# Four of eight row pairs of w_up by seven products in five chunks, with part of their sums made by transfers in HBM

## The chip, the cores and the metric

The kernel runs on one core of a Trainium2 chip. The metric is the device time of one execution in microseconds. Engines are named as in the profile: PE multiplies matrices, DVE and ACT work elementwise, POOL (GpSimd) does small work and issues some of the transfers, SP issues most transfers. Each engine takes its instructions in the order written; engines wait for each other by semaphores only.

## The reference

One layer on 256 tokens of width 2048, all in float32, one batch, one layer deep:

```
h = rmsnorm(x) * g1;  p = h @ W_in               # 2048 x 4160, columns for the two attentions
A = dilated-window attention, 8 heads of 128 ;  B = latent attention, 8 heads
x = x + rmsnorm(concat(A, B) @ W_out) * g2       # 2048 x 2048
h = rmsnorm(x) * g3
u = square(relu(h @ W_up))                       # 2048 x 8192
x = x + rmsnorm(u @ W_down) * g4                 # 8192 x 2048
```

The change is in the product with W_up, and in work that goes on beside the attention stages.

## The kernel before, in words

**Three passes.** A product of float32 matrices is made from parts: each operand is split into `hi`, its float32r rounding, and `lo`, the rest, and hi·hi, hi·lo and lo·hi are added in PSUM. A weight tile comes from HBM into one of five buffers `raw`; ACT writes `hi` (line 293, or 297 where a column of norm gains is multiplied in), DVE writes `lo` (line 294 or 298). There are eight buffers each of `hi` and `lo`; the class `Weights` emits a tile's load and split six tiles ahead of its use. So a split waits for the product eight tiles back, and a load on SP waits for the split five loads back.

**The product with w_up.** The 8192 columns are done in 16 chunks of 1024. A chunk runs over 16 row tiles of 128 (`k`), two token blocks `b` and two column halves, and adds into four PSUM banks; a plain tile takes 2 × 2 × 3 = 12 matmuls of 512 columns. Two neighbouring row tiles form a 2 × 2 block product, which Winograd's form of Strassen's scheme does with seven block products instead of eight: 21 matmuls instead of 24. In chunks 1 to 15 the pairs 0, 1 and 2 (row tiles 0 to 5) are done so, steps ("w", 0), ("w", 1), ("w", 2) of `UP_STEPS`; row tiles 6 to 15 are plain steps ("k", k). In chunk 0 all are plain.

**Right sums.** With the pair's rows `a` = (a0, a1) and `b` = (b0, b1), halves of 512 columns, the seven products need a0, b, t = (a0 + a1, a1 + b1) and u = (a0 + a1 + b1, a0 + a1 + b1 + b0). Both rows are loaded to a staging tile `ab` (of which there is one), by POOL except for the very first pair; DVE makes t and u in three additions (lines 345, 349, 350), and four tiles are split: a0 (512 columns), b, u, t.

**Left sums.** `left_sums` makes, once, the four sums of each pair of tiles of the normalized input hT, and writes the gain-scaled values back over hT; so from chunk 1 on, rows 0 to 5 need no gain in the split. This happens during the second half of chunk 0. The sums lie in the tile `st`.

**Closing.** Four further PSUM banks `m` collect the products that are shared between outputs; after the last pair of a chunk `close` combines them on DVE, and while the next chunk runs `up_evac` adds them to the accumulators (line 909), applies relu on ACT, transposes on PE (line 287) and squares on ACT.

**Order.** The program is written out by one pass of Python. `Flow` keeps a clock that counts the planned cost of the matmuls issued; side chains (generators) give waiting times with `yield`, and are resumed when that clock has passed. So an operation's place in an engine's order follows from planned times, while the engines themselves run as their waits allow. In the attention stages POOL has only a few small operations: the powers that make 1/rms (`rstd_pre`, `rstd_kv`, `rstd_q`, `rstd_pw`, line 485) and one memset.

Of the kernel before, what the change touches and what calls it, by code (L numbers as in the profile page):

```python
# [18 lines left out]
F32 = mybir.dt.float32  # L19
# [7 lines left out]
P = 128  # L27
# [11 lines left out]
FF = 4 * D  # L39
# [53 lines left out]
D_UP, UP_STEP = 1.8, 2.2  # L93


N_SEVEN, SUMS_AHEAD = 3, 2
UP_STEPS = [("k", k) for k in range(6, 11)]
for _i, _n in enumerate(((11, 12), (13,), (14, 15))):
    UP_STEPS += [("w", _i)] + [("k", k) for k in _n]


DOWN_SEVEN = ((7, 11, 13, 17, 19, 23, 25, 29), (4, 7, *range(9, 28, 2)))
# [148 lines left out]
def layer(nc, tc, io):  # L251
# [76 lines left out]
    def up_weight(j, k):  # L328
        return io["w_up"][k * P:(k + 1) * P, j * CW:(j + 1) * CW]

    late = {}

    def seven(load, targets):

# [28 lines left out]
    def seven_up(j, kp):  # L363
        def load():
            if j == FF // CW - 1 and kp:
                return [weights.load(up_weight(j, 2 * kp + i), CW, f"raw_w{j}_{kp}{i}") for i in range(2)]
            return load_two(late["ab"], nc.gpsimd if (j, kp) > (1, 0) else nc.sync,
                            io["w_up"][2 * kp * P:(2 * kp + 2) * P, j * CW:(j + 1) * CW])
# [30 lines left out]


    wide_u, after = [], 0
    for j in range(FF // CW):
        wide_u.append([])
        for what, k in [("k", k) for k in range(KD)] if j == 0 else UP_STEPS:
            if what == "k":
                ts = [weights.plan(up_weight(j, k), 1, CW, gcol[:, 8 + k:9 + k])]
# [124 lines left out]
    def prelude():  # L531
# [14 lines left out]
        nc.vector.reduce_sum(ss0, ss0h, axis=mybir.AxisListType.X)  # L546
        rstd0.append(rstd_of(ss0, NB, D, "pre"))

    def tables():

        yield D_TAB[0]
        nc.scalar.dma_start(out=pos_i, in_=io["pos"])
        nc.scalar.dma_start(out=cst, in_=io["consts"])
        yield D_TAB[1]
        pos_f = con.tile([P, NB], F32, name="pos_f")
        nc.vector.tensor_copy(pos_f, pos_i)
        ang = pa.tile([P, 2, NB, 96], F32, tag="qkT", bufs=2, name="ang")
# [12 lines left out]
        yield 4.0  # L570
        nc.scalar.activation(trig, ang, AF.Sin)
# [77 lines left out]

    pre = flow.start(prelude())  # L650
    tab = flow.start(tables())
    heads, evacs = [], []
    for half in range(2):
        qkv = {}
# [250 lines left out]
    def up_evac(j, b, i, acc, order, more=None):  # L905

        yield UP_STEP * order
        if more is not None:
            nc.vector.tensor_tensor(out=acc, in0=acc, in1=more, op=OP.add)
            yield 1.6  # L910
        r = late["up"].tile([P, 512], F32, tag="r", bufs=2, name=f"r{j}_{b}")
        nc.scalar.activation(r, acc, AF.Relu, scale=rstd2[b])
        yield D_UP if j > 1 else 2 * D_UP
        t = bank(i, f"rt{j}_{b}")
        for k in range(4):
            transpose(t[:, k * P:(k + 1) * P], r[:, k * P:(k + 1) * P])
# [41 lines left out]
    def left_sums(kp):  # L958

        up, k, tt = late["up"], 2 * kp, nc.vector.tensor_tensor  # L960
        f, q = [late["c"][:, i * 512:(i + 1) * 512] for i in range(2)]
        hs = [t[:, k:k + 2, :].rearrange("p k s -> p (k s)") for t in hT]
        tt(out=f, in0=hs[0].bitcast(F32), in1=hs[1].bitcast(F32), op=OP.add)
# [3 lines left out]
        st = [late["st"][:, i * 512:(i + 1) * 512] for i in (2 * kp, 2 * kp + 1)]  # L967
        yield 3.0
        for t, x in ((hs, f), (st, q)):
            nc.scalar.activation(t[0], x, AF.Copy)  # L970
        yield 1.5
        for t, x in ((hs, f), (st, q)):
            tt(out=t[1], in0=x, in1=t[0].bitcast(F32), op=OP.subtract)
        sums.append([[t[:, i * P:(i + 1) * P] for t in st] for i in range(4)])
        yield 0.5

    def all_sums():
        for kp in range(N_SEVEN - 1):
            yield from left_sums(kp)
        yield 8.0  # L980
        yield from left_sums(N_SEVEN - 1)

    def three(out, a, w, first, last):

# [3 lines left out]
    def seven_products(ts, left, accs, m, first, last):  # L988

        (a11, a12, a22), (s3, s1, s2, s4) = left  # L990
        prods = ((a11, 0, 0, 1), (a12, 1, 0, (0, 0)), (s4, 1, 1, (0, 1)), (s2, 2, 0, 6), (a22, 2, 1, (1, 0)),
                 (s3, 3, 1, 7), (s1, 3, 0, 5))
        for p, (a, i, half, to) in enumerate(prods):
            w = weights.get(ts[i])
# [21 lines left out]
    for j in range(FF // CW):  # L1016
# [9 lines left out]
        for t, b in order:  # L1026
            what, k, tiles = steps[t]
            if (j, t, b) == (0, 8, 0):
                flow.finish(*res)
                late["po"].release()  # L1030
                mix.release()
                late["up"] = pool("up", "right")
                late["st"] = late["up"].tile([P, 3 * CW], F32R, tag="st", bufs=1, name="st")
                for n in ("ab", "c"):
                    late[n] = late["up"].tile([P, 2 * CW], F32, name=n)
                flow.start(all_sums())
# [3 lines left out]
            if j == 1 and what == "w":  # L1040
                flow.until(lambda: len(sums) > k)
            if what == "k":
                w = weights.get(tiles[0])
                h_done(k, b)
                for n in range(2):
                    c = slice(n * 512, (n + 1) * 512)
                    three(accs[b, n], [tok(hT[x], k, b) for x in range(2)], [w[x][:, 0, c] for x in range(2)], t == 0, t == len(steps) - 1)
                    if j == 0 and t == len(steps) - 1:
                        evac.append(flow.start(up_evac(n, b, at[b, n], accs[b, n], 2 * b + n - 0.25 * (2 * b + n))))
                    flow.pump()  # L1050
                if b == NB - 1:
                    weights.free(tiles[0])
                continue

            first, last = k == 0, k == N_SEVEN - 1
# [208 lines left out]
```

## Time and profile before

| | |
|---|---|
| median of three runs | 1052.88 us (1051.48 to 1053.32) |
| the profiled execution | 1052.05 us, span 1050.3 us, mean granted clock 0.998 |
| busy: PE, DVE, ACT, POOL | 1039.0, 811.0, 625.4, 61.5 us |
| transfers | 229.34 MB, 218 GB/s over the span |
| attention stages and w_out | to about 363 us |
| w_up, chunk 0 | about 363 to 407 us, then a chunk each 43.4 us |

A row of the page's groups names line, engine, operation, what is written and read, the count, then busy time in us and the mean of one in ns, then idle time before it and what ended that. In a timeline the first two columns are start and length in us; a bracket gives the idle time of that engine before it and what ended it.

### The profile page before, as it was taken

What the parts mean: (1) busy time and instruction counts of PE and PEld (TensorE: products, weight loads), DVE (VectorE), ACT (ScalarE), POOL (GpSimd) and SP (SyncE); (2) the same over time, 40 slices, a digit from 0 to 9 for tenths busy, and PEclk for the clock granted to TensorE, in tenths of its full rate; (3) what the DMA queues carried; (4) which work ended last, traced back from release to release, by engine and by line L of the source; (5) the groups of instructions that cost most, each with busy time, mean ns of one, the idle gap of its engine ahead of it and who ended that gap; (6) DMA issues with size and microseconds to landing.
All of it is one profiled execution on the core that took longest, in us unless ns stands there. A gap on an engine that the chain in (4) does not pass through costs nothing.

```text
span 1050.3 us, 13459 instructions
## 1 busy us (share of the span) xinstructions
PE 1039.0 (99%) x4854; PEld 865.9 (82%) x4854; DVE 811.0 (77%) x1080; ACT 625.4 (60%) x834; POOL 61.5 (6%) x116
## 2 busy tenths in 40 slices
PE   9999999999999999999999999999999999999996
PEld 6888899888888788888888888888888888888885
DVE  6676536577557679879888798887899978989995
ACT  6675436565555467666665666666567564766661
POOL 0000000000000000010000000000000001112100
PEclk9999999999999999999999999999999999999999
DMA  8975447454447295646556465469788767788952
GB/s 298 371 230 155 140 127 239 141 166 155 141 170 234 77 344 174 224 143 238 194 189 201 145 234 194 151 227 319 246 276 315 267 223 259 268 300 313 381 186 81
DMA packets 80643, 229.34 MB, mean 218 GB/s; under 512 B 7616, under 2 KB 12224, under 8 KB 80192
## 3 DMA queue, kind: packets, MB, share of 16 engines
q1 hardware_dynamic: 65888, 176.45, 50.3%
q0 software_dynamic: 14112, 51.39, 14.2%
q8 instruction: 38, 0.62, 0.2%
q10 hardware_dynamic: 576, 0.64, 0.2%
q14 instruction: 29, 0.24, 0.1%
HBM read 212.72 MB, written 15.73 MB: 218 GB/s over the span
## 4 chain that ended last, share of the span: by engine, by line
PE 96%; DVE 1%; DMA 1%; issue 1%; ACT 0%; POOL 0%; DVEq 0%; POOLq 0%; ACTq 0%
PE y L283 26%; PE acc_u L283 26%; PE acc_o L283 8%; PE m L283 5%; PE md L283 5%; PE acc_v L283 4%; PE acc_qk L283 4%; PE acc_ckv L283 2%; PE acc_ukv L283 2%; PE acc_q L283 2%; PE acc_cq L283 2%; PE acc_k L283 2%; PE acc_uq L283 2%; PE rt L287 1%; PE sc_b L283 1%
## 5 line engine op out<-in xcount | busy, mean ns | idle before, releaser
L294 DVE TENSOR_TENSOR lo<-raw,hi 128x1024 fp32r<-128x1024 f32 (+3 forms) x213 | 241.7, 1152 | 91.5 <-ACT hi L293 90.7
L293 ACT ACTIVATE hi<-raw 128x1024 fp32r<-128x1024 f32 (+3 forms) x213 | 209.5, 999 | 77.6 <-PE y L283 20.8
L283 PE MATMUL acc_u<-hi,hT_hi 128*128 128x512 f32 x386 | 153.3, 397 | 0.0
L283 PE MATMUL acc_u<-hi,hT_lo 128*128 128x512 f32 x386 | 151.0, 391 | 0.4 <-DVE hT_lo L294 0.4
L283 PE MATMUL acc_u<-lo,hT_hi 128*128 128x512 f32 x386 | 150.7, 391 | 0.0
L283 PE MATMUL y<-hi,uhi 128*128 128x512 f32 x376 | 146.8, 390 | 0.0
L283 PE MATMUL y<-hi,ulo 128*128 128x512 f32 x376 | 146.5, 390 | 0.0
L283 PE MATMUL y<-lo,uhi 128*128 128x512 f32 x376 | 146.5, 390 | 0.0
L298 DVE SCALAR_TENSOR_TENSOR lo<-raw,gcol,hi 128x1024 fp32r<-128x1024 f32 x86 | 107.6, 1280 | 11.2 <-ACT hi L297 11.0
L297 ACT ACTIVATE hi<-raw,gcol 128x1024 fp32r<-128x1024 f32 x86 | 97.8, 1151 | 24.8 <-PE acc_u L283 10.9
L283 PEld LDWEIGHTS acc_u<-hi,hT_lo 128*128 128x128 f32 x386 | 72.5, 188 | 16.1 <-DVE hT_lo L294 0.8
L283 PEld LDWEIGHTS acc_u<-lo,hT_hi 128*128 128x128 f32 x386 | 72.6, 188 | 14.2
L283 PEld LDWEIGHTS acc_u<-hi,hT_hi 128*128 128x128 f32 x386 | 72.6, 188 | 13.9
L283 PEld LDWEIGHTS y<-hi,uhi 128*128 128x128 f32 x376 | 70.6, 188 | 14.6
L283 PEld LDWEIGHTS y<-hi,ulo 128*128 128x128 f32 x376 | 70.6, 188 | 14.6
L283 PEld LDWEIGHTS y<-lo,uhi 128*128 128x128 f32 x376 | 70.6, 188 | 14.5
L283 PE MATMUL acc_o<-hi,mixT_hi 128*128 128x512 f32 x128 | 51.9, 405 | 0.0
L294 DVE TENSOR_TENSOR lo<-st_down,hi 128x1024 fp32r<-128x1024 f32 x40 | 48.1, 1220 | 4.0 <-ACT hi L293 3.8
L283 PE MATMUL acc_o<-hi,mixT_lo 128*128 128x512 f32 x128 | 50.2, 392 | 0.0
L283 PE MATMUL acc_o<-lo,mixT_hi 128*128 128x512 f32 x128 | 50.0, 391 | 0.0
L293 ACT ACTIVATE hi<-ab 128x512 fp32r<-128x512 f32 (+1 forms) x38 | 32.0, 842 | 29.3 <-PE acc_u L283 24.4
L293 ACT ACTIVATE hi<-st_down 128x1024 fp32r<-128x1024 f32 x40 | 42.1, 1053 | 11.1 <-PE y L283 9.5
(322 smaller groups left out, 1986.3 us busy)
## 6 DMA issues: line engine op xcount, KB each, us to landing
raw<-in_w_down SPq DMA_DIRECT2D x88, 512.0 KB, 6.0
raw<-in_w_up SPq DMA_DIRECT2D x86, 512.0 KB, 4.5
raw<-in_w_in SPq DMA_DIRECT2D x55, 512.0 KB, 5.0
ab<-in_w_up POOLq DMA_DIRECT2D x36, 512.0 KB, 5.0
raw<-in_w_out SPq DMA_DIRECT2D x32, 512.0 KB, 4.3
ab_down<-in_w_down POOLq DMA_DIRECT2D x20, 512.0 KB, 6.4
ukeep<-ulo SPq DMA_DIRECT2D x15, 512.0 KB, 7.2
ulo<-ukeep POOLq DMA_DIRECT2D x15, 512.0 KB, 5.4
```

Source lines behind the costliest of these rows:

```text
L283: nc.tensor.matmul(out, a, b, start=start, stop=stop)
L287: nc.tensor.transpose(out, a, ident)
L293: nc.scalar.activation(hi, src, AF.Copy)
L294: nc.vector.tensor_tensor(out=lo, in0=src, in1=hi.bitcast(F32), op=OP.subtract)
L297: nc.scalar.activation(hi, src, AF.Copy, scale=g)
L298: nc.vector.scalar_tensor_tensor(out=lo, in0=src, scalar=g, in1=hi.bitcast(F32), op0=OP.mult, op1=OP.subtract)
```

## The change

1. Chunks 1 to 5 do four pairs by seven products, 0, 1, 2 and 3, and eight plain tiles, 8 to 15, in the order `k8 k9 k10 k11 p0 k12 w1 k13 w2 p3 k14 k15`. Chunks 6 to 15 keep three pairs and their order.
2. In these five chunks the pairs 0 and 3 (steps `p`) have their right sums t and u prepared in HBM: for each of the ten pairs, `prepare` issues two plain copies on SP (t = a; u = b1 twice) and four adding transfers on POOL (a1 and b1 onto t; b0 onto u; then t's first half onto both halves of u). It starts at 50 us of planned time, a pair each 24 us, with 12 us between the dependent steps. A `p` step then has no additions on DVE: its four tiles are loaded through `raw` by SP (a0, b, and the kept u and t) and split like plain tiles.
3. A fourth pair of left sums is made, in a tile `st2` that lies where uT10 will be written after chunk 5; left sums of pairs 2 and 3 start 18 us of planned time after those of 0 and 1. As this scales rows 6 and 7 too, their splits need no gain from chunk 1 on.
4. All staging loads of `ab` go on POOL.

```diff
-N_SEVEN, SUMS_AHEAD = 3, 2
-UP_STEPS = [("k", k) for k in range(6, 11)]
...
+UP_STEPS = {0: [("k", k) for k in range(KD)]}
+for _j in range(1, 6):
+    UP_STEPS[_j] = steps_of("k8 k9 k10 k11 p0 k12 w1 k13 w2 p3 k14 k15")
...
+SCALED = {j: range(8) for j in range(1, NUP)}
+PREP = [(j, k) for j in UP_STEPS for w, k in UP_STEPS[j] if w == "p"]
+D_PREP = (50.0, 24.0, 12.0)
...
+    sums_kept = {jk: dram.tile([P, 2 * CW], F32, name=f"sums{jk[0]}_{jk[1]}") for jk in PREP}
...
+            elif what == "p":
+                kept = sums_kept[j, k]
+                ts = [weights.plan(src, 1, n) for src, n in (
+                    (up_weight(j, 2 * k)[:, :512], 512), (up_weight(j, 2 * k + 1), CW),
+                    (kept[:, CW:], CW), (kept[:, :CW], CW))]
...
+    def prepare(j, kp):
+
+        H, kept = 512, sums_kept[j, kp]
+        t, u = kept[:, :CW], kept[:, CW:]
+        a, b = [io["w_up"][(2 * kp + i) * P:(2 * kp + i + 1) * P, j * CW:(j + 1) * CW] for i in range(2)]
+
+        def twice(x):
+            return x.unsqueeze(1).to_broadcast([P, 2, H])
+
+        nc.sync.dma_start(out=t, in_=a)
+        nc.sync.dma_start(out=u.rearrange("p (k n) -> p k n", k=2), in_=twice(b[:, H:]))
+        yield D_PREP[2]
+        nc.gpsimd.dma_start(out=t[:, :H], in_=a[:, H:], accum_op=OP.add)
+        nc.gpsimd.dma_start(out=t[:, H:], in_=b[:, H:], accum_op=OP.add)
+        nc.gpsimd.dma_start(out=u[:, H:], in_=b[:, :H], accum_op=OP.add)
+        yield D_PREP[2]
+        nc.gpsimd.dma_start(out=u.rearrange("p (k n) -> p k n", k=2), in_=twice(t[:, :H]), accum_op=OP.add)
+
+    def prepare_all():
+
+        yield D_PREP[0]
+        for jk in PREP:
+            yield from prepare(*jk)
+            yield D_PREP[1] - 2 * D_PREP[2]
...
+    flow.start(prepare_all())
...
+            elif j == 10:
+                t2 = late["up"].tile([P, CW], F32, tag="uT10", bufs=1, name="uT10")
...
+        sp, i0 = (late["st"], 2 * kp) if kp < 3 else (late["st2"], 2 * kp - 6)
...
+                late["st2"] = late["up"].tile([P, CW], F32R, tag="uT10", bufs=1, name="st2")
+                flow.start(some_sums((0, 1)))
+                flow.start(some_sums((2, 3), 18.0))
```

Where this puts instructions, at two places. First POOL in the attention stages. Before, `rstd_pre` to `rstd_pw` follow each other:

```order
L485 TENSOR_TENSOR rstd_pre_601<-t_pre_600,neg_half_82 128x2
L485 TENSOR_TENSOR rstd_kv_1705<-t_kv_1704,neg_half_82 128x2
L485 TENSOR_TENSOR rstd_q_1923<-t_q_1922,neg_half_82 128x2
L710 MEMSET krT_1891 128x512
L485 TENSOR_TENSOR rstd_pw_3002<-t_pw_3001,neg_half_82 128x2
```

Now, around the same `rstd_kv` and `rstd_q` (the tile sums3_0 is that of chunk 3, pair 0; L580 to L582 are a pair's first three adding transfers, L584 the fourth):

```order
L580 DMA sums3_0_74<-in_w_up 128x512
L581 DMA sums3_0_74<-in_w_up 128x512
L582 DMA sums3_0_74<-in_w_up 128x512
L504 TENSOR_TENSOR rstd_kv_1744<-t_kv_1743,neg_half_92 128x2
L584 DMA sums3_0_74<-sums3_0_74 128x2x512
L504 TENSOR_TENSOR rstd_q_1965<-t_q_1964,neg_half_92 128x2
L580 DMA sums3_3_75<-in_w_up 128x512
```

Each of the small operations now stands behind adding transfers, which wait on POOL for the transfers they build on.

Second DVE in chunk 3, between the second and the third pair that have their sums made on chip. Before (t3_2 and u3_2 are the sums of the third pair, lo196 is row tile 13, lo197 to lo200 that pair's splits, then come tiles 14 and 15):

```order
L294 TENSOR_TENSOR lo195_4569<-t3_1_4482,hi195_4568 128x1024
L345 TENSOR_TENSOR t3_2_4580<-ab_3501 128x1024
L349 TENSOR_TENSOR u3_2_4581<-t3_2_4580,ab_3501 128x512
L350 TENSOR_TENSOR u3_2_4581<-u3_2_4581,ab_3501 128x512
L298 SCALAR_TENSOR_TENSOR lo196_4588<-raw196_4585,gcol_69,hi196_4587 128x1024
L294 TENSOR_TENSOR lo197_4604<-ab_3501,hi197_4603 128x512
L294 TENSOR_TENSOR lo198_4620<-ab_3501,hi198_4619 128x1024
L294 TENSOR_TENSOR lo199_4627<-u3_2_4581,hi199_4626 128x1024
L294 TENSOR_TENSOR lo200_4637<-t3_2_4580,hi200_4636 128x1024
L298 SCALAR_TENSOR_TENSOR lo201_4649<-raw201_4646,gcol_69,hi201_4648 128x1024
L298 SCALAR_TENSOR_TENSOR lo202_4661<-raw202_4658,gcol_69,hi202_4660 128x1024
```

Now, from the same sums on:

```order
L359 TENSOR_TENSOR t3_2_4652<-ab_3571 128x1024
L363 TENSOR_TENSOR u3_2_4653<-t3_2_4652,ab_3571 128x512
L364 TENSOR_TENSOR u3_2_4653<-u3_2_4653,ab_3571 128x512
L311 SCALAR_TENSOR_TENSOR lo198_4660<-raw198_4657,gcol_69,hi198_4659 128x1024
L307 TENSOR_TENSOR lo199_4670<-ab_3571,hi199_4669 128x512
L307 TENSOR_TENSOR lo200_4686<-ab_3571,hi200_4685 128x1024
L307 TENSOR_TENSOR lo201_4693<-u3_2_4653,hi201_4692 128x1024
L307 TENSOR_TENSOR lo202_4703<-t3_2_4652,hi202_4702 128x1024
L307 TENSOR_TENSOR lo203_4715<-raw203_4712,hi203_4714 128x512
L307 TENSOR_TENSOR lo204_4727<-raw204_4724,hi204_4726 128x1024
L307 TENSOR_TENSOR lo205_4745<-raw205_4742,hi205_4744 128x1024
L307 TENSOR_TENSOR lo206_4754<-raw206_4751,hi206_4753 128x1024
```

The four splits lo203 to lo206 of the prepared pair 3 have come after those of the third pair, ahead of tiles 14 and 15; they read `raw`, and no sums stand before them.

More of the change, by code (lines that the diff above doesn't have):

```diff
@@ L93, with steps_of @@
 D_UP, UP_STEP = 1.8, 2.2
-N_SEVEN, SUMS_AHEAD = 3, 2
-UP_STEPS = [("k", k) for k in range(6, 11)]
-for _i, _n in enumerate(((11, 12), (13,), (14, 15))):
-    UP_STEPS += [("w", _i)] + [("k", k) for k in _n]
+SUMS_AHEAD = 2
+NUP = FF // CW
+def steps_of(text):
+    return [(s[0], int(s[1:])) for s in text.split()]
+UP_STEPS = {0: [("k", k) for k in range(KD)]}
+for _j in range(1, 6):
+    UP_STEPS[_j] = steps_of("k8 k9 k10 k11 p0 k12 w1 k13 w2 p3 k14 k15")
+for _j in range(6, NUP):
+    UP_STEPS[_j] = steps_of("k6 k7 k8 k9 k10 w0 k11 k12 w1 k13 w2 k14 k15")
+SCALED = {j: range(8) for j in range(1, NUP)}
+PREP = [(j, k) for j in UP_STEPS for w, k in UP_STEPS[j] if w == "p"]
+D_PREP = (50.0, 24.0, 12.0)
 DOWN_SEVEN = ((7, 11, 13, 17, 19, 23, 25, 29), (4, 7, *range(9, 28, 2)))
@@ L366, in load @@
                 return [weights.load(up_weight(j, 2 * kp + i), CW, f"raw_w{j}_{kp}{i}") for i in range(2)]
-            return load_two(late["ab"], nc.gpsimd if (j, kp) > (1, 0) else nc.sync,
-                            io["w_up"][2 * kp * P:(2 * kp + 2) * P, j * CW:(j + 1) * CW])
+            return load_two(late["ab"], nc.gpsimd, io["w_up"][2 * kp * P:(2 * kp + 2) * P, j * CW:(j + 1) * CW])
         return seven(load, lambda: [late["up"].tile([P, CW], F32, tag="T", bufs=2, name=f"{n}{j}_{kp}") for n in "tu"])
@@ L401, in layer @@
     wide_u, after = [], 0
-    for j in range(FF // CW):
+    for j in range(NUP):
         wide_u.append([])
-        for what, k in [("k", k) for k in range(KD)] if j == 0 else UP_STEPS:
+        for what, k in UP_STEPS[j]:
             if what == "k":
-                ts = [weights.plan(up_weight(j, k), 1, CW, gcol[:, 8 + k:9 + k])]
+                g = () if k in SCALED.get(j, ()) else (gcol[:, 8 + k:9 + k],)
+                ts = [weights.plan(up_weight(j, k), 1, CW, *g)]
+            elif what == "p":
[3 more added lines that the diff above has]
+                    (kept[:, CW:], CW), (kept[:, :CW], CW))]
             else:
@@ L966, in left_sums @@
         four_sums(q, f)
-        st = [late["st"][:, i * 512:(i + 1) * 512] for i in (2 * kp, 2 * kp + 1)]
+        sp, i0 = (late["st"], 2 * kp) if kp < 3 else (late["st2"], 2 * kp - 6)
+        st = [sp[:, i * 512:(i + 1) * 512] for i in (i0, i0 + 1)]
         yield 3.0
@@ L975, in left_sums, with some_sums @@
         yield 0.5
-    def all_sums():
-        for kp in range(N_SEVEN - 1):
+    def some_sums(kps, after=0.0):
+        yield after
+        for kp in kps:
             yield from left_sums(kp)
-        yield 8.0
-        yield from left_sums(N_SEVEN - 1)
     def three(out, a, w, first, last):
@@ L993, in seven_products @@
         for p, (a, i, half, to) in enumerate(prods):
-            w = weights.get(ts[i])
+            w = [x[:, 0, :] if len(x.shape) == 3 else x for x in weights.get(ts[i])]
             in_m = isinstance(to, int)
@@ L1035, in layer @@
                     late[n] = late["up"].tile([P, 2 * CW], F32, name=n)
-                flow.start(all_sums())
+                late["st2"] = late["up"].tile([P, CW], F32R, tag="uT10", bufs=1, name="st2")
+                flow.start(some_sums((0, 1)))
+                flow.start(some_sums((2, 3), 18.0))
             if (j, t, b) == (FF // CW - 1, 4, 0):
@@ L1039, in layer @@
                 u_next = split_u(0, 0)
-            if j == 1 and what == "w":
+            if what != "k":
                 flow.until(lambda: len(sums) > k)
@@ L1053, in layer @@
                 continue
-            first, last = k == 0, k == N_SEVEN - 1
+            pairs = [s[1] for s in steps if s[0] != "k"]
+            first, last = k == pairs[0], k == pairs[-1]
             if first:
```

## The prediction

> **What bounds the kernel now.** I read the page first: the busy shares and the chain that ended last.
>
> ```profile
> PE 1039.0 (99%) x4854; PEld 865.9 (82%) x4854; DVE 811.0 (77%) x1080; ACT 625.4 (60%) x834; POOL 61.5 (6%) x116
> PE 96%; DVE 1%; DMA 1%; issue 1%; ACT 0%; POOL 0%; DVEq 0%; POOLq 0%; ACTq 0%
> ```
>
> PE holds 96% of the chain. Matmuls overlap, so a busy PE could still hide gaps; the starts decide. In the chain in order of time, the columns are start, length, what; these are the closing steps of w_up chunks 1, 2 and 3:
>
> ```profile
> 439.45 10.88 PE acc_u L283 x48
> 482.85 10.88 PE acc_u L283 x48
> 526.25 10.88 PE acc_u L283 x48
> ```
>
> 48 matmuls of 512 columns in 10.88 us are 0.2267 us each, with no gap, and chunks follow each other every 43.40 us (482.85 − 439.45, 526.25 − 482.85).
>
> Next, busy time by stage, to see what the other engines and the DMA engines have left (the two last columns are DMA share and GB/s):
>
> ```profile
> 60.00:300.00 240.00, 239.81 (x1268) 207.77 (x1267) 144.31 (x300) 130.72 (x239) 2.57 (x4) 1.00 0.51 156
> 300.00:400.00 100.00, 99.60 (x455) 81.70 (x454) 68.93 (x97) 57.38 (x89) 4.22 (x5) 1.00 0.67 228
> 400.00:620.00 220.00, 220.00 (x1010) 182.17 (x1009) 189.88 (x204) 138.80 (x159) 16.36 (x30) 1.00 0.59 195
> ```
>
> The columns are PE, PEld, DVE, ACT, POOL, then the granted clock, 1.00. PE idles 0.2 us of 240 and 0 of 220. So only fewer matmuls shorten this kernel, and anything added costs time only once it outlasts the lead of the weights over PE. How long that lead is, before MLP: a load's issue on SP against the first product that reads it (w_ukv, w_out), and the last narrow w_in split on DVE against its use:
>
> ```profile
> 172.68 7.34 SPq L175 DMA_DIRECT2D raw<-in_w_ukv  x4
> 202.39 2.72 PE acc_ukv L283 x12
> 220.43 9.00 SPq L175 DMA_DIRECT2D raw<-in_w_out  x5
> 253.32 4.12 PE acc_o L283 x18
> 161.42 0.76 DVE L294 TENSOR_TENSOR lo<-raw,hi 128x576 fp32r<-128x576 f32 x1 [0.84 <-ACT hi L293]
> 175.30 1.59 PE acc_ckv L283 x12
> ```
>
> Loads are issued 29.7 and 32.9 us before use; the split of the latest 576-wide tile ends 13.1 us ahead (175.30 − 162.18). I take 13 us as the lead there.
>
> **The change, part by part.**
>
> *Products.* Chunks 1 to 5 take four pairs in seven products instead of three. A pair in eight costs 2 tiles × 2 token blocks × 2 halves × 3 passes = 24 matmuls, in seven 21. Five chunks × 3 = 15 fewer, no transpose added: 15 × 0.2267 = **−3.40 us**, all on the bound engine. [...] Were loading the pace, 15 × 865.9/4854 = 2.7 us would go; no run has shown it, and 48 starts in 10.88 us speak for 3.40.
>
> *DVE and ACT in the chunks.* Chunk 3 of the kernel before, DVE in time: the sums for the third pair, the scaled split of tile 13, and that pair's four splits; then POOL's two loads for those sums, and PE's start of tile 13:
>
> ```profile
> 510.50 1.23 DVE L345 TENSOR_TENSOR t<-ab 128x1024 f32<-128x1024 f32 x1 [2.06 <-DMA ab<-in_w_up]
> 513.10 1.28 DVE L298 SCALAR_TENSOR_TENSOR lo<-raw,gcol,hi 128x1024 fp32r<-128x1024 f32 x1
> 514.30 1.82 DVE L294 TENSOR_TENSOR lo<-ab,hi 128x512 fp32r<-128x512 f32 x2
> 518.30 3.67 DVE L298 SCALAR_TENSOR_TENSOR lo<-raw,gcol,hi 128x1024 fp32r<-128x1024 f32 x3
> 503.91 0.54 POOL L360 DMA_DIRECT2D ab<-in_w_up  x1 [11.65 <-DVE lo L294]
> 506.46 0.54 POOL L360 DMA_DIRECT2D ab<-in_w_up  x1 [2.01 <-DVE lo L294]
> 518.77 2.72 PE acc_u L283 x12
> ```
>
> By starts, sums take 2.60 us (510.50 to 513.10), a scaled split 1.20, four splits of a pair 4.00 (514.30 to 518.30). Per chunk DVE loses one set of sums and two scaled splits and gains four splits: −2.60 − 2.40 + 4.00 = −1.0 us. ACT swaps two 1024-wide copies for 512 + 3 × 1024 columns, about 3.5 − 2 = +1.5 us at the mean of the row below, in 138.80 of 220 us busy. Both are off PE's path.
>
> ```profile
> L293 ACT ACTIVATE hi<-raw 128x1024 fp32r<-128x1024 f32 (+3 forms) x213 | 209.5, 999 | 77.6 <-PE y L283 20.8
> ```
>
> The narrowest lead is here: tile 13 is split at 514.38 and used at 518.77, 4.4 us, because its split stands behind sums that wait for POOL's loads (issued at 506.46, there 4.0 us later). Those loads wait for the pair before to leave the staging tile, which waits for the split buffer eight tiles back. Before, that is the fifth tile of the chunk, and from its release to tile 13 PE has 21 + 24 + 21 = 66 matmuls; after, it is the third, with 12 + 21 + 12 + 21 = 66. The same lead, 0 us. Behind it the prepared pair 3 needs 4.0 (third pair) + 0.6 of DVE within tile 13 and the third pair's 33 matmuls, 7.5 us: the lead grows. At the chunk's edge the sums of the next fresh pair now stand between the first and second closing add of the last chunk (2.60 us), but the first add no longer waits behind two of that pair's splits; I count 0.
>
> *A fourth left sum* in chunks 0 and 1, the cost of one on DVE:
>
> ```profile
> 390.66 0.68 DVE L973 TENSOR_TENSOR hT_lo<-c,hT_hi 128x512 fp32r<-128x512 f32 x1
> 391.86 0.68 DVE L963 TENSOR_TENSOR c<-hT_hi,hT_lo 128x512 f32<-128x512 f32 x1
> 394.23 1.28 DVE L298 SCALAR_TENSOR_TENSOR lo<-raw,gcol,hi 128x1024 fp32r<-128x1024 f32 x1
> 432.37 6.07 DVE L298 SCALAR_TENSOR_TENSOR lo<-raw,gcol,hi 128x1024 fp32r<-128x1024 f32 x5
> ```
>
> 2.37 (391.86 to 394.23) + 1.20 (390.66 to 391.86) = 3.57 us, against 2.60 of right sums that chunk 1 sheds before its first pair: +1.0 us in front of splits that stay over 3 us ahead; five splits in a row at 432.37 show DVE not starved. 0 us; uncovered, 1.0.
>
> *The preparation.* Ten pairs, each two plain 512 KB copies HBM to HBM on SP, then three adding transfers of 256 KB and one of 512 KB on POOL. POOL in turn loses eight staging loads in chunks 1 to 5, SP two. The trace has no adding and no HBM-to-HBM transfer. Nearest rows, the queues' totals and landings:
>
> ```profile
> q1 hardware_dynamic: 65888, 176.45, 50.3%
> q0 software_dynamic: 14112, 51.39, 14.2%
> raw<-in_w_up SPq DMA_DIRECT2D x86, 512.0 KB, 4.5
> ukeep<-ulo SPq DMA_DIRECT2D x15, 512.0 KB, 7.2
> uT<-xkeep SPq DMA_DIRECT2D x4, 512.0 KB, 12.4
> ```
>
> q1 moved 176.45 MB in 50.3% of 1050.3 us, 334 GB/s, q0 345 GB/s. 10.5 MB copied and 13.1 MB added are 31 + 38 = 69 us of all 16 engines at least. Upwards I scale by landings: 7.2 / 4.5 = 1.6 for a write to HBM gives 110 us; 12.4 / 4.5 = 2.8, the slowest row, 190 us. Idle in 60 to 300 are 0.49 × 240 = 118 us. An add reads two operands and writes HBM, so the row of the write is nearest: I take 1.6, which fits into the idle time and 13 us of lead: **0 us**, bounds 0 and the second rival's price. Below nothing it can't go, as it frees nothing.
>
> POOL waits in order, and its few small operations now stand behind adds:
>
> ```profile
> 180.90 0.70 POOL L485 TENSOR_TENSOR rstd_kv<-t_kv,neg_half 128x2 f32<-128x2 f32 x1 [117.24 <-DVE t_kv L484]
> L779 ACT ACTIVATE kb<-acc_ukv,rstd_kv x8: 467/476/483, 210.1 to 239.3; 128x256 f32<-128x256 f32 x8
> 205.78 0.69 POOL L485 TENSOR_TENSOR rstd_q<-t_q,neg_half 128x2 f32<-128x2 f32 x1 [24.18 <-DVE t_q L484]
> L786 ACT ACTIVATE qb<-acc_uq,rstd_q x8: 557/582/584, 218.7 to 253.4; 128x384 f32<-128x384 f32 x8
> 348.56 0.55 POOL L485 TENSOR_TENSOR rstd_post<-t_post,neg_half 128x1 f32<-128x1 f32 x1 [27.37 <-DVE t_post L484]
> ```
>
> rstd_kv is ready 28.5 us before its first reader, rstd_q 12.2 us. A pair makes POOL wait twice, for the copies and for the first three adds, 12 us of planned time after each; at landings of 7 to 12 us it doesn't fall behind. The last add stands ahead of rstd_post, so it is issued by 349; chunk 1 begins at 406.9 (439.45 + 10.88 − 43.40), and its first prepared pair is the first made.
>
> *Sum.* The profiled execution took 1052.05 us; −3.40 gives 1048.65. It lies 0.83 below the median of the runs, 1052.88, from which the same step gives 1049.48. I say **1049.2**.
>
> **The rivals.**
>
> *Given back in the chunks.* DVE at the chunk edges or the fourth left sum is late by tenths: 0.3 us at five chunks and 1.0 in chunk 1 return 2.5 of the 3.4, about 1051.7. For it: DVE is 86% busy there (189.88 of 220); against: the leads above.
>
> *Adds crowd out the weights: slower.* Place: 60 to 300 us. From a factor of (118 + 13) / 69 = 1.9 on, the added transfers outlast idle time and lead. At 2.8 there are 190 − 118 = 72 us too many; if weight loads bear half, 36 − 13 = 23 us reach PE: about 1073; at 2.2, half of 34 less 13, 4 us: 1053. The same slow adds would hold POOL, rstd_q first. For it: nothing here measured an add. Against: the adds have time until 400 us, so they need not land soon. [...]
>
> *The third pair's loads land late: slower.* SP now loads 7.9 MB per chunk where it loaded 5.2, and POOL's loads run beside that. From 8.4 us (4.0 + 4.4) on PE waits for tile 13; at 12.4, 4.0 us in each of five chunks: 1069. Against: the four loads of pair 3 are issued before these.
>
> *It doesn't do what it says:* the prepared sums are late and SP waits for them. By the places above that takes adds slow enough for the second rival.
>
> **How the numbers follow.** A measurement of this kernel tells about 0.2%, 2.1 us, from no change. Forecast 0.64 (1048.0 to 1050.3), given back 0.16 (1050.5 to 1052.9), crowded out 0.16 (1053 to 1073), late landings 0.04 (1053 to 1069). Faster is under 1050.8: 0.63 of the forecast and 0.02 of the second, 0.65. Within is up to 1055.0: 0.01 of the forecast, 0.14 of the second and 0.04 of the last two, 0.19. Slower is their rest, 0.16. The range, 1047.8 to 1055.5, takes the first two whole and the lower edge of the last two.
>
> **What would show it.** Right: chunks 1 to 5 follow each other in 42.72 us (43.40 − 0.68), chunk 6 on in 43.40; PE idle still near 0.2 us in 60 to 300; DMA share there near 0.51 + 110/240 = 0.97 at 1.6, or 0.80 at 1.0. Wrong: gaps on PE before acc_o with ACT waiting for raw; rstd_q or rstd_pw late behind adds; tile 13 waiting for DVE.

## The result: slower by 11 us

| | before | after |
|---|---|---|
| median of four executions of each kernel (lowest to highest) | 1052.63 us (1051.48 to 1053.32) | 1063.63 us (1063.12 to 1066.42) |
| profiled execution | 1052.05 us | 1066.42 us |
| ratio | | 1.0111, 95% interval 1.0091 to 1.0131 |

The forecast was 1049.2 us, between 1047.8 and 1055.5. It was wrong in sign. (A slip in the description above: w_up has 8192 / 1024 = 8 chunks, 0 to 7, not 16. So chunks 6 and 7 keep three pairs. No number of the prediction hangs on it.)

The page of the kernel after, busy times and the chain that ended last:

```profile
PE 1041.5 (98%) x4839; PEld 863.4 (81%) x4839; DVE 811.2 (76%) x1083; ACT 631.1 (59%) x846; POOL 94.5 (9%) x148
PE 72%; DVE 12%; DMA 8%; issue 4%; ACT 3%; DVEq 0%; POOL 0%; POOLq 0%; ACTq 0%; SPq 0%
```

The trace has 4839 matmuls where it had 4854: the 15 are gone. But PE's share of the chain fell from 96% to 72%; DVE, DMA and ACT have come in. Busy time by stage tells where (columns as in the prediction: PE, PEld, DVE, ACT, POOL, clock, DMA share, GB/s); the attention stages and then chunks 1 to 5, after:

```profile
60.00:300.00 240.00, 239.81 (x1266) 207.68 (x1265) 143.86 (x299) 130.69 (x238) 38.79 (x43) 1.00 0.92 251
400.00:660.00 260.00, 247.83 (x1122) 200.25 (x1121) 213.60 (x233) 162.69 (x194) 12.90 (x24) 1.00 0.64 214
```

In 60 to 300 us, where 39 of the 40 adding transfers are issued, PE idles 0.19 us as before. In the chunks it idles 12.2 us of 260, where it idled none (260.00 before). What PE waited for there (columns: sum, times, longest, in us):

```profile
PE rt L300 <- ACT r L957: 7.7, 6, 1.6
PE acc_u L296 <- DVE c L1055: 3.5, 3, 1.3
```

Both are work at the edge of a chunk: the transposition of the finished chunk, which waits for the relu on ACT (line 957), and the first products of the new chunk, which write the banks that were `m` and wait for `close` on DVE (line 1055) to have read them. In PE's timeline from 400 to 660 us, 12 starts are late by more than 0.15 us, 14.1 us in all; the kernel before has none. From the fourth group of transpositions of chunk 0 to that of chunk 5 it takes 233.2 us, before 220.4. These 12.8 us (14.1 of late starts and 2.1 of starts late by less than 0.15, minus the 3.4 of the 15 matmuls) and 1.6, by which the first product of w_up starts later (355.80 against 354.17), are the 14.4 us between the two profiled executions.

The 1.6 us are not the transfers': they are there in a kernel without them (355.68), and not in the old kernel with them (354.15). They arise at the program's start. In this execution the first products start 0.43 us apart until about 10.3 us, where the execution of before has them 0.23 apart from 5.45 us on; after, then before:

```profile
5.63 0.63 PE L296 MATMUL acc_qk<-hi,xT_lo 128*128 128x512 f32 x1
6.06 0.63 PE L296 MATMUL acc_qk<-hi,xT_hi 128*128 128x512 f32 x1
...
5.45 0.40 PE L283 MATMUL acc_qk<-hi,xT_lo 128*128 128x512 f32 x1
5.68 0.45 PE L283 MATMUL acc_qk<-hi,xT_hi 128*128 128x512 f32 x1
```

The run with splits four tiles ahead, below, is the same program as the changed kernel up to chunk 1; there w_up starts at 354.03. So the changed program runs with and without the 1.6 us; whether it meets them more often than the old one is not shown.

### The profile page after: what moved, and what is told of

It is laid out like the page before. It is cut to its first block, busy times and chain, and to the rows that moved or that the text cites. A ratio compares the mean times of both kernels' runs of the same rounds, so it can differ in the third digit from the quotient of the medians.

```text
span 1064.6 us, 13618 instructions
## 1 busy us (share of the span) xinstructions
PE 1041.5 (98%) x4839; PEld 863.4 (81%) x4839; DVE 811.2 (76%) x1083; ACT 631.1 (59%) x846; POOL 94.5 (9%) x148
## 4 chain that ended last, share of the span: by engine, by line
PE 72%; DVE 12%; DMA 8%; issue 4%; ACT 3%; DVEq 0%; POOL 0%; POOLq 0%; ACTq 0%; SPq 0%
PE y L296 25%; PE acc_o L296 8%; PE acc_u L296 6%; PE md L296 5%; PE acc_qk L296 4%; DVE lo L307 4%; PE acc_v L296 4%; DMA raw<-in_w_up 4%; PE acc_ckv L296 2%; DVE lo L311 2%; DMA ab<-in_w_up 2%; PE acc_ukv L296 2%; PE acc_q L296 2%; PE acc_cq L296 2%; PE acc_k L296 2%
## 5 line engine op out<-in xcount | busy, mean ns | idle before, releaser
L307 DVE TENSOR_TENSOR lo<-raw,hi 128x1024 fp32r<-128x1024 f32 (+3 forms) x257 | 288.0, 1142 | 96.5 <-ACT hi L306 95.8
L306 ACT ACTIVATE hi<-raw 128x1024 fp32r<-128x1024 f32 (+3 forms) x257 | 250.8, 992 | 101.4 <-PE y L296 20.8
L296 PE MATMUL acc_u<-hi,hT_hi 128*128 128x512 f32 x356 | 142.4, 400 | 3.6 <-DVE c L1055 3.5
L296 PE MATMUL acc_u<-lo,hT_hi 128*128 128x512 f32 x356 | 139.1, 391 | 0.8 <-DVE lo L311 0.8
L296 PE MATMUL acc_u<-hi,hT_lo 128*128 128x512 f32 x356 | 139.2, 391 | 0.4 <-DVE hT_lo L307 0.4
L311 DVE SCALAR_TENSOR_TENSOR lo<-raw,gcol,hi 128x1024 fp32r<-128x1024 f32 x72 | 91.8, 1281 | 27.1 <-ACT hi L310 26.6
L310 ACT ACTIVATE hi<-raw,gcol 128x1024 fp32r<-128x1024 f32 x72 | 82.5, 1149 | 32.8 <-DMA raw<-in_w_up 18.3
L296 PEld LDWEIGHTS acc_u<-hi,hT_hi 128*128 128x128 f32 x356 | 66.9, 188 | 18.8 <-DVE c L1055 6.2
L296 PEld LDWEIGHTS acc_u<-hi,hT_lo 128*128 128x128 f32 x356 | 66.8, 188 | 15.1 <-DVE hT_lo L307 0.8
L296 PE MATMUL m<-hi,st 128*128 128x512 f32 x156 | 56.5, 389 | 0.0
L306 ACT ACTIVATE hi<-st_down 128x1024 fp32r<-128x1024 f32 x40 | 42.1, 1052 | 11.1 <-PE y L296 9.5
```

Of the source, the lines that this page charges most:

```text
L296: nc.tensor.matmul(out, a, b, start=start, stop=stop)
L306: nc.scalar.activation(hi, src, AF.Copy)
L307: nc.vector.tensor_tensor(out=lo, in0=src, in1=hi.bitcast(F32), op=OP.subtract)
L310: nc.scalar.activation(hi, src, AF.Copy, scale=g)
L311: nc.vector.scalar_tensor_tensor(out=lo, in0=src, scalar=g, in1=hi.bitcast(F32), op0=OP.mult, op1=OP.subtract)
```

## One edge, row by row

The edge between chunks 3 and 4. Before, DVE's two closing adds (a row with x2 holds the second and third), and PE's first two transpositions:

```profile
534.75 0.69 DVE L909 TENSOR_TENSOR acc_u<-acc_u,c 128x512 f32<-128x512 f32 x1
536.48 1.29 DVE L909 TENSOR_TENSOR acc_u<-acc_u,c 128x512 f32<-128x512 f32 x2
...
537.21 0.69 ACT L912 ACTIVATE r<-acc_u,rstd_pre 128x512 f32<-128x512 f32 x1 [1.04 <-DVE acc_u L909]
...
536.98 0.60 PE L287 MATMUL rt<-ident,r 128*128 128x128 f32 x4
539.50 0.60 PE L287 MATMUL rt<-ident,r 128*128 128x128 f32 x4
```

The first add stands 2.23 us ahead of the first transposition; the second relu is done at 537.90, 1.60 us before the transposition that reads it. That 1.60 us is all the slack the second transposition had, and it had no more at the other edges behind chunks 1 to 5 (the first transposition had 0.8). After, the same place, DVE, ACT and PE:

```profile
533.54 3.86 DVE L311 SCALAR_TENSOR_TENSOR lo<-raw,gcol,hi 128x1024 fp32r<-128x1024 f32 x3 [0.77 <-ACT hi L310]
537.32 2.27 DVE L1055 TENSOR_TENSOR c<-m,c 128x512 f32<-128x512 f32 x3
540.23 2.96 DVE L307 TENSOR_TENSOR lo<-raw,hi 128x512 fp32r<-128x512 f32 x3
543.11 0.69 DVE L954 TENSOR_TENSOR acc_u<-acc_u,c 128x512 f32<-128x512 f32 x1
543.71 1.21 DVE L359 TENSOR_TENSOR t<-ab 128x1024 f32<-128x1024 f32 x1
...
546.29 1.22 DVE L307 TENSOR_TENSOR lo<-raw,hi 128x1024 fp32r<-128x1024 f32 x1
547.43 1.29 DVE L954 TENSOR_TENSOR acc_u<-acc_u,c 128x512 f32<-128x512 f32 x2
...
532.35 2.42 ACT L310 ACTIVATE hi<-raw,gcol 128x1024 fp32r<-128x1024 f32 x2 [0.90 <-DMA raw<-in_w_up]
542.78 1.06 ACT L306 ACTIVATE hi<-raw 128x1024 fp32r<-128x1024 f32 x1 [1.86 <-DMA raw<-sums]
548.15 0.69 ACT L957 ACTIVATE r<-acc_u,rstd_pre 128x512 f32<-128x512 f32 x1 [3.63 <-DVE acc_u L954]
...
544.63 0.60 PE L300 MATMUL rt<-ident,r 128*128 128x128 f32 x4
548.89 0.66 PE L300 MATMUL rt<-ident,r 128*128 128x128 f32 x4 [1.61 <-ACT r L957]
```

Two things have happened. Between the first and the second add now stand the sums of the next fresh pair and a split, 4.3 us (543.11 to 547.43) where there were 1.7: 2.6 us. And the first add itself stands only 1.5 us ahead of the first transposition, 0.7 less. In front of it DVE has the splits of the next chunk's tiles 9 to 11 (from 533.54), `close`, and three splits of prepared pair 0, and works through them without a break. Its last wait, 0.77 us, is for ACT's half of tile 9, and that waits for the tile's load. (ACT waits for a kept sum too, at 542.78, but the turn of that tile on DVE comes only at 546.29, so here it holds up nothing.) 1.60 − 2.6 − 0.7 = −1.7 us, and PE's second transposition is late by 1.74 us.

Why the loads are late, in SP's queue and on DVE, after:

```profile
502.61 4.50 SPq L188 DMA_DIRECT2D raw<-sums  x2
519.83 13.30 SPq L188 DMA_DIRECT2D raw<-in_w_up  x8
534.85 1.59 SPq L188 DMA_DIRECT2D raw<-sums  x2
...
515.93 1.23 DVE L359 TENSOR_TENSOR t<-ab 128x1024 f32<-128x1024 f32 x1 [2.21 <-DMA ab<-in_w_up]
518.53 1.28 DVE L311 SCALAR_TENSOR_TENSOR lo<-raw,gcol,hi 128x1024 fp32r<-128x1024 f32 x1
```

The five buffers `raw` hold row tile 13 and the four tiles of prepared pair 3. So the load of tile 14 waits for tile 13's split, which stands behind the third pair's sums and ends at 519.81; SP issues at 519.83. The row's eight loads are tiles 14 and 15, the next chunk's 8 to 11, and the first two of its pair 0; each behind the first is issued when the next split on DVE ends, the last at 532.80. The kept sums of pair 0 come after them, 9.8 us before the first transposition.

## Experiments

The letters of an order: k a plain row tile, w a pair with fresh sums, p a prepared pair.

**The transfers alone**, in the kernel before, with nothing that reads their result:

```diff
+PREP = [(j, k) for j in range(1, 6) for k in (0, 3)]
...
+    flow.start(prepare_all())
```

> The kernel before plus the twenty copies and forty adding transfers, at the same planned times; nothing reads what they make. Theory (the loss lies in chunks 1 to 5, where the splits of the prepared pairs fill the five raw buffers, the loads behind them come late, and the closing adds and relu stand behind splits that wait for loads): 1052 to 1054 us, PE idle under 1 us in 60 to 300. Rival (the transfers crowd out the weight loads or hold POOL): at least 1058 us, with PE idle in 60 to 360.

Measured: 1051.88 us against 1052.72, ratio 0.9998 (0.9988 to 1.0007). Its stage of 60 to 300 us:

```profile
60.00:300.00 240.00, 239.81 (x1267) 207.67 (x1267) 144.72 (x300) 131.30 (x239) 38.81 (x43) 1.00 0.91 251
```

The DMA share goes from 0.51 to 0.91, POOL's busy time from 2.57 to 38.81 us, and PE doesn't notice.

**The order without the transfers.** The prepared pairs load rows of w_up in place of the kept sums, so the sums are left out of the computation:

```diff
-                    (kept[:, CW:], CW), (kept[:, :CW], CW))]
+                    (up_weight(j, 2 * k + 1), CW), (up_weight(j, 2 * k), CW))]
...
-    flow.start(prepare_all())
```

> The changed kernel without the copies and adds; where it would load the kept sums it loads rows of w_up of the same size, so the sums of the prepared pairs are left out. Theory (late loads in the chunks): as the changed kernel, 1061 to 1065 us, with PE waiting at the chunk edges for relu by 1.6 us each. Rival (the transfers cost the time): 1048 to 1052 us.

Measured: 1061.36 us, ratio 1.0082 (1.0067 to 1.0097). The same waits, at the same place:

```profile
PE rt L300 <- ACT r L956: 6.1, 4, 1.6
PE acc_u L296 <- DVE c L1054: 2.4, 3, 1.4
```

So the loss is the chunks' and not the transfers'. By the medians it is 2.3 us smaller than with them; the late starts sum to 10.1 us instead of 14.1. Why the kept sums cost these few us more than rows of w_up in their place was not settled.

**Fresh pair at the edge**, prepared pair 3 left in its place (the other prepared pair is now pair 1):

```diff
-    UP_STEPS[_j] = steps_of("k8 k9 k10 k11 p0 k12 w1 k13 w2 p3 k14 k15")
+    UP_STEPS[_j] = steps_of("k8 k9 k10 k11 w0 k12 p1 k13 w2 p3 k14 k15")
```

> Only the order of the steps in chunks 1 to 5: k8 k9 k10 k11 w0 k12 p1 k13 w2 p3 k14 k15, so that the first pair after a chunk's edge has fresh sums and takes no raw buffer. Theory (late loads of the prepared pair behind the edge): the waits at the edges go, 1049 to 1052 us. Rival (DVE has too much to do for four pairs, in whatever order): no more than 3 us better than the changed kernel, 1060 to 1064 us.

Measured: 1053.24 us, ratio 1.0009 (1.0000 to 1.0019), a little above what the theory gave. Four late starts in 400 to 660 us, 3.5 us in all. The closing adds on DVE at the edge of chunks 3 and 4, and PE's first two transpositions:

```profile
536.60 0.69 DVE L954 TENSOR_TENSOR acc_u<-acc_u,c 128x512 f32<-128x512 f32 x1
537.20 1.22 DVE L307 TENSOR_TENSOR lo<-t,hi 128x1024 fp32r<-128x1024 f32 x1
538.33 1.29 DVE L954 TENSOR_TENSOR acc_u<-acc_u,c 128x512 f32<-128x512 f32 x2
...
538.12 0.60 PE L300 MATMUL rt<-ident,r 128*128 128x128 f32 x4
540.64 0.60 PE L300 MATMUL rt<-ident,r 128*128 128x128 f32 x4
```

The adds are 1.7 us apart again, as before the change: with a fresh pair at the edge, no sums stand between them. The first still stands only 1.5 us ahead of the first transposition, as in the change; the second transposition is on time all the same.

**A buffer of its own for u** of each prepared pair, so that a prepared pair holds three of the five `raw` instead of four (order unchanged):

```diff
...
-                ts = [weights.plan(src, 1, n) for src, n in (
+                own = lambda name: late["up"].tile([P, CW], F32, tag="uT11", bufs=1, name=name)
+                ts = [weights.plan(src, 1, n, None, own if i == 2 else None) for i, (src, n) in enumerate((
...
```

> One of the four tiles of each prepared pair (its sum u) is loaded into a buffer of its own, where uT11 is written later, so a prepared pair takes three raw buffers instead of four. Theory (raw ring): about a third to a half of the loss goes, 1055 to 1060 us. Rival (the order of DVE's work, not the loads): 1062 to 1065 us.

Measured: 1058.24 us, ratio 1.0057 (1.0040 to 1.0073); seven late starts, 6.6 us in all:

```profile
PE rt L300 <- ACT r L958: 3.8, 4, 1.6
PE acc_u L296 <- DVE c L1056: 1.1, 2, 0.9
```

One buffer more gives half of the loss back. That the ring of five is a part of it is shown by this run; that it is the whole of it is not.

**Two further orders**, both with a fresh pair first: three plain tiles after the last pair, and fresh pairs first and last:

```diff
+    UP_STEPS[_j] = steps_of("k8 k9 k10 k11 w0 p1 k12 w2 p3 k13 k14 k15")
+    UP_STEPS[_j] = steps_of("k8 k9 k10 k11 w0 p1 k12 p2 k13 w3 k14 k15")
```

> Order of chunks 1 to 5: k8 k9 k10 k11 w0 p1 k12 w2 p3 k13 k14 k15: fresh sums first as in the run before, and three plain tiles instead of two behind the last prepared pair. Theory (after a prepared pair the ring of five raw buffers needs time to run ahead again before the closing subtractions are due): the two or three waits of about 1 us for the closing subtractions that the run with fresh sums first still has go, 1049 to 1051.5 us. Rival (DVE has no time left for the closing with four pairs): 1052.5 us or more, as with fresh sums first.

> Order of chunks 1 to 5: k8 k9 k10 k11 w0 p1 k12 p2 k13 w3 k14 k15: fresh sums first and last, both prepared pairs in the middle, so that during the last pair nothing leaves or enters the raw ring but the loads of the plain tiles behind it. Theory: no waits at the chunk edges, the whole 3.4 us, 1048.5 to 1050.5 us, unless the two prepared pairs with one plain tile between them starve their own products. Rival (DVE has no time left): 1052.5 us or more.

Measured: 1052.41 (ratio 0.9996, 0.9986 to 1.0005) and 1051.98 us (0.9993, 0.9984 to 1.0003) against 1053.10. Both fall between what the theory and what the rival gave. Each has two late starts left, 2.2 and 2.4 us in all, the last of them at the edge of chunks 1 and 2; from there on chunks 2 to 5 take 42.7 us each: the 42.72 of the prediction.

**Splits planned four tiles ahead** instead of six in chunks 1 to 5, in the changed kernel, so that fewer splits stand in front of the edge's work:

```diff
+            if j and (t, b) == (0, 0):
+                weights.ahead = 4 if j < 6 else W_AHEAD
```

> The changed kernel in its own order of steps, with tiles emitted four instead of six ahead in chunks 1 to 5, so that the closing subtractions and adds stand ahead of two splits that they now stand behind. Theory in the form that it is the place behind waiting splits that costs: 1056 to 1061 us. If the loads as such are too late for the products: the same or slower, 1063 us or more, with PE waiting for lo.

Measured: 1063.45 us, ratio 1.0098 (1.0074 to 1.0121), no better than the change. PE's waits have only moved:

```profile
PE acc_u L296 <- DVE lo L311: 8.5, 5, 2.4
PE rt L300 <- ACT r L957: 3.9, 1, 3.9
```

Now once in each chunk a product waits for its split. A shorter lead is no cure for late loads.

**Fresh first and last, and the own buffer**, the two cures together:

```diff
+    UP_STEPS[_j] = steps_of("k8 k9 k10 k11 w0 p1 k12 p2 k13 w3 k14 k15")
...
+                own = lambda name: late["up"].tile([P, CW], F32, tag="uT11", bufs=1, name=name)
```

> As the order with fresh sums first and last, and the sum u of each prepared pair in a buffer of its own besides. Theory: nothing or a few tenths better than without it, 1048.5 to 1050 us, since the raw ring no longer holds anything up. Rival (the ring still short): at least 1 us better than without it.

Measured: 1050.66 us against 1053.10, ratio 0.9980 (0.9970 to 0.9989). This is 1.3 us below the same order without the buffer, where the theory gave a few tenths and the rival, a ring still short, at least 1 us; the intervals of the two ratios overlap a little. One late start is left, 1.2 us at the edge of chunks 0 and 1, where ACT has a left sum of pair 2 ahead of the relu:

```profile
407.62 0.63 ACT L1019 ACTIVATE hT_hi<-c 128x512 fp32r<-128x512 f32 x1 [4.09 <-DVE c L1013]
```

**The left sums of pairs 2 and 3 later** by 10 us of planned time, with that order, and with the three-tiles-after order, both with the own buffer:

```diff
-                flow.start(some_sums((2, 3), 18.0))
+                flow.start(some_sums((2, 3), 28.0))
```

> The order and the buffer of e11_fresh_last_own, and one number more: the left sums of pairs 2 and 3 are planned 28 us after those of pairs 0 and 1 are set off, where it was 18, so that their work on DVE and ACT no longer stands ahead of the relu at the edge of chunks 0 and 1. Theory (the one gap left, 1.2 us at 409 us, is ACT waiting for the left sums of pair 2): the gap goes, 1.2 us less than e11_fresh_last_own, 1049.0 to 1050.0 us. Rival (the relu there is late for the loads of the first prepared pair, not for the sums): same time as e11_fresh_last_own, 1050.7, with a gap of about 1 us still at 409. A loss: pair 2's left sums are now late for its own products, PE waits inside chunk 1, over 1051.

> The order of e5_three_after (three whole tiles after the last pair, which is a prepared one) with the own buffer and the late left sums of e12_late_left_sums. Theory (what matters is that no prepared pair and no fresh pair's sums stand within two tiles of the edge): no gap in chunks 2 to 5, 1049.0 to 1050.2 us. Rival (the place of the last prepared pair counts by itself, because its four buffers bunch the loads of the next chunk): gaps of 0.5 to 2 us return at the edges, 1051 to 1053.

Measured: 1053.90 us (ratio 1.0008, 0.9999 to 1.0017) and 1053.59 us (1.0004, 0.9995 to 1.0012) against 1053.09. The wait at 409 us went, as the theory said, but the time rose, to over 3 us above what was expected. In the first of them PE waits at the end of chunk 1 instead, for closing subtractions on DVE, and then runs slowly for a while (PE's timeline):

```profile
448.95 0.79 PE L296 MATMUL acc_u<-hi,hT_hi 128*128 128x512 f32 x1 [1.35 <-DVE c L1056]
449.54 0.63 PE L296 MATMUL acc_u<-lo,hT_hi 128*128 128x512 f32 x1
449.97 0.63 PE L296 MATMUL acc_u<-hi,hT_lo 128*128 128x512 f32 x1
```

Its late starts sum to 3.9 us instead of 1.2. The two medians differ by 3.2 us (0.28% by the ratios), so this accounts for most of it. In the second three starts are late, 3.6 us in all, none of them after 455 us. It looks as if the delay of ten planned us had moved the collision to another edge; no run isolates that.

**No prepared pair**: four fresh pairs, nothing prepared.

```diff
+    UP_STEPS[_j] = steps_of("k8 k9 k10 k11 w0 k12 w1 k13 w2 k14 w3 k15")
```

> No prepared pair: all four pairs of chunks 1 to 5 take fresh sums on DVE (order k8 k9 k10 k11 w0 k12 w1 k13 w2 k14 w3 k15), and nothing is prepared in HBM. Theory (the prepared sums spare DVE 5.2 us of a chunk; without them DVE would need about 41.4 of 42.72 us, with waits in between): PE waits for splits and closing adds in every chunk, chunks follow each other in 43.5 to 45.5 us, 1054 to 1064. Rival (DVE still fits, and the prepared pairs cost more by their four buffers than they spare): chunks of 42.7 us, 1049 to 1051, as good as e11_fresh_last_own without a transfer more.

Measured: 1093.50 us, ratio 1.0380 (1.0363 to 1.0397). Chunks 2 to 5 take 50.5 to 51.5 us each. The direction was expected, the size was not. Busy time in two stretches at one edge:

```profile
500.00:504.00 4.00, 1.80 (x8) 1.14 (x7) 3.97 (x6) 2.00 (x2) 0.00 (x0) 1.00 0.68 212
506.00:511.00 5.00, 4.34 (x11) 3.20 (x11) 4.97 (x7) 0.69 (x1) 0.54 (x1) 0.50 0.76 246
```

DVE is busy without a break (3.97 of 4.00, 4.97 of 5.00) while PE waits for it, and after the wait PE's granted clock is 0.50. Of the 43 us by which matmuls start late in 400 to 665 us, 29.6 are waits and 13.6 such slow matmuls. DVE's work in one of these chunks is 41.4 us (41.43 busy in 520 to 571 us), which leaves almost nothing of 42.72 for its waits. So the preparation does carry something: without it, in this order, DVE can't keep up.

**Two letters exchanged.** The sharpest test of the explanation: prepared pair 0 stays right behind the edge, with the same sums between the closing adds; only the last pair is now a fresh one, so that pair 2's four buffers are asked for a pair earlier.

```diff
-    UP_STEPS[_j] = steps_of("k8 k9 k10 k11 p0 k12 w1 k13 w2 p3 k14 k15")
+    UP_STEPS[_j] = steps_of("k8 k9 k10 k11 p0 k12 w1 k13 p2 w3 k14 k15")
```

> The changed kernel with the last two pairs of chunks 1 to 5 exchanged in kind: k8 k9 k10 k11 p0 k12 w1 k13 p2 w3 k14 k15 in place of ... w2 p3 k14 k15. Prepared pair 0 stays first, right behind the edge; only the last pair is now a fresh one, which holds no raw buffer. Theory (both are needed for the loss: the last prepared pair, whose four buffers put off the loads of k14, k15, k8 to k11 and p0 and bunch them, and prepared pair 0, whose four splits then stand late ahead of the relu): most of the loss goes, gaps on PE between 400 and 660 us of 2 to 6 us, 1052 to 1056 us. Rival (prepared pair 0 behind the edge is enough by itself): as the changed kernel, gaps of 10 to 14 us, 1060 to 1064.

Measured: 1050.06 us (1048.36 to 1050.46) against 1052.68, ratio 0.9972 (0.9959 to 0.9984). All of the loss is gone, and more: the theory gave 1052 to 1056. Busy time by stage, then DVE, ACT, SP and PE at the edge of chunks 3 and 4:

```profile
400.00:660.00 260.00, 260.00 (x1194) 215.16 (x1193) 227.94 (x248) 174.29 (x204) 14.03 (x26) 1.00 0.70 231
...
506.12 1.28 DVE L311 SCALAR_TENSOR_TENSOR lo<-raw,gcol,hi 128x1024 fp32r<-128x1024 f32 x1
533.00 0.69 DVE L954 TENSOR_TENSOR acc_u<-acc_u,c 128x512 f32<-128x512 f32 x1
537.32 1.29 DVE L954 TENSOR_TENSOR acc_u<-acc_u,c 128x512 f32<-128x512 f32 x2
...
538.04 0.69 ACT L957 ACTIVATE r<-acc_u,rstd_pre 128x512 f32<-128x512 f32 x1 [3.63 <-DVE acc_u L954]
...
507.42 15.47 SPq L188 DMA_DIRECT2D raw<-in_w_up  x8
523.84 1.52 SPq L188 DMA_DIRECT2D raw<-sums  x2
...
536.78 0.60 PE L300 MATMUL rt<-ident,r 128*128 128x128 f32 x4
539.31 0.60 PE L300 MATMUL rt<-ident,r 128*128 128x128 f32 x4
```

Tile 13's split no longer stands behind sums: it ends at 507.40, and SP begins the same run of eight loads at 507.42, 29.4 us before the first transposition instead of 24.8; the kept sums follow 12.9 us before it instead of 9.8. The first closing add stands 3.8 us ahead of it instead of 1.5. The second still comes 4.3 us after the first, and its relu is done 0.6 us before PE needs it: 1.60 − 2.6 + 1.55 = 0.55. PE has no late start in 400 to 660 us.

Taken together: without the sums between the closing adds (the third experiment) most of the loss goes, though the first add is as late as in the change; with these sums but with earlier loads all of it goes. The waits for relu need both. The waits for `close` don't need the sums: of their 4.5 us of late starts the third experiment still has 2.3.

## Why the prediction was wrong, step by step

**Products: right.** −3.40 us. In the kernel with two letters exchanged, chunks 2 to 5 take 42.72 us each, from chunk 0's fourth transposition to chunk 5's it is 217.0 us against 220.4, and the sum holds: 1052.05 − 3.40 + 1.85 (its first product of w_up starts at 356.02 instead of 354.17, most of it again from the program's start) = 1050.50, its profiled execution 1050.46. The other value weighed there, 2.7 us with weight loading (PEld) as the pace, falls with it.

**The chunk's edge: the step that failed.** "At the chunk's edge the sums of the next fresh pair now stand between the first and second closing add of the last chunk (2.60 us), but the first add no longer waits behind two of that pair's splits; I count 0." The place was right and the 2.60 us too. The rest was argued, not read: the slack that the 2.60 us had to fit into, 1.60 us, stood in the trace of before and was not looked up. The gain that was to offset them does not follow from the order either: between `close` and the first add DVE has three splits as before, 2.9 us, only of other tiles. It came out as +1.55 us only where the loads are early. In the change, it is −0.7 us, and the term put at 0 measured 1.7 us at this edge.

**What was left out: the ring of `raw`.** Tile 13's split was followed to one of its readers, PE, and its lead there found unchanged; this was right in chunks 2 to 5. (In chunk 1 PE waits for this split once, 0.8 us: it stands behind sums that wait 3.0 us for POOL's load, as the rival on late landings had it.) But SP's next load waits for the same split, because a prepared pair's four tiles fill the rest of a ring of five, and the loads after that wait for the splits that come next on DVE, so all of them are late together. The rival on late loads has the sentence that hid this: "the four loads of pair 3 are issued before these". So they are, and that is why the loads behind them are late.

**The fourth left sum: 0, right for the change's order,** as the run with two letters exchanged shows, where the left sums stand at the same place (from the fourth transposition of chunk 0 to that of chunk 1 it is 46.1 us, before 46.8). In another order, that of the two cures together, the left sums of pair 2 cost 1.2 us; the 3.9 us of the run that delayed them are not traced to them.

**The preparation: 0 us, right,** by the first experiment. DMA share rose by 0.40 of 240 us, 96 us of 16 engines, a factor of 1.4 on the 69 us at the queue's own rate; 1.6 was taken. The small operations on POOL cost PE nothing. The median landing of w_out's loads went from 4.3 to 7.5 us, and that too was covered.

**The rivals.** *Given back in the chunks* named the place and not the size: 0.3 us an edge, where chunks 2 to 5 are 2.2 to 3.2 us longer than 42.72. With 1.6 us of slack read from the trace, this rival would have been worth 1.7 us at each edge as soon as the loads are late, and its sign would have been open. *Adds crowd out the weights* fell with the first experiment. *The prepared sums are late* fell too: the last adding transfer is issued at 322.8 us, some 80 us before chunk 1.

## What to carry to other kernels

Where work is put in front of an instruction that the bound engine waits for, its price is its length minus the slack of that instruction, and the slack is one subtraction in the trace of before. A tile that passes through a ring of buffers has two readers: the engine that uses it, and the load that waits for its place; follow both. And where a program is written in a fixed order, exchange two neighbours before giving the change up: here the exchange of two letters is worth some 14 us (ratios of 1.0111 and 0.9972).

## What the runs showed of the hardware that was not expected

Adding transfers from HBM to HBM ran beside weight loads at a DMA share of 0.91 with PE idle 0.19 us of 240, as without them, and an issue of one kept POOL busy about 0.9 us: (38.81 − 2.57) us over the 43 − 4 instructions that POOL has more in 60 to 300 us.

After some waits the traces of three runs show PE's matmuls 0.43 us apart instead of 0.2267, at a granted clock near half, for several us. In the kernel without prepared pairs, a wait of 2.8 us from 501.8 us on, and one of 0.7 us soon after it, were followed by matmuls 0.43 us apart to about 511 us, at a granted clock of 0.50 in 506 to 511 us. In the run with the late left sums, waits of 0.7 and 1.35 us within 3.0 us did the same for some 3 us, at a granted clock of 0.58 in 449 to 453 us. In the run with splits four tiles ahead, the wait of 3.9 us for the relu, up to 634.3 us, was followed by this spacing to about 639 us, at 0.57 in 632 to 640 us. In the changed kernel, waits of 0.9 and 1.35 us from 630.6 us on did not bring it, with 1.00 granted in 630 to 636 us, and neither did a single wait of 2.4 us in the run with splits four tiles ahead, after which the next matmuls start 0.23 to 0.33 us apart. So waits that add up to 2 us can cost more than their length, though they need not: in the run with the late left sums, 2.06 us of waits came to 3.9 us of late starts. What decides between the two is not shown.
